# Keeping product 2's weights in dead activation tiles for product 3's sum, in the second projection of an FFN

## The chip, the cores and the metric

The kernel runs on one core of a Trainium2 chip. The metric is the device time of one execution in microseconds, as the median of several executions. Engines: PE (TensorE, with PEld for its weight loads), DVE (VectorE), ACT (ScalarE), POOL (GpSimd, used here to issue accumulating DMAs) and SP (SyncE, used here to issue DMAs).

## What is computed

A hybrid encoder trunk of two layers on 512 tokens of width 1024, all in float32. Each layer is a half-step FFN, a pair of gated mixers, and another half-step FFN; a final norm follows. Cut to what matters here:

```python
D_MODEL = 1024; SEQ = 512; DEPTH = 2; D_FF = 2816

def swiglu(x, w_in, w_out):
    gu = x @ w_in                      # 1024 -> 2 x 2816
    g, u = jnp.split(gu, 2, axis=-1)
    return (jax.nn.silu(g) * u) @ w_out  # 2816 -> 1024, "the second projection"

for l in range(DEPTH):
    x = x + 0.5 * swiglu(rms_norm(x, ffn1_norm[l]), ffn1_w_in[l], ffn1_w_out[l])
    x = x + mixer(rms_norm(x, mix_norm[l]), ...)
    x = x + 0.5 * swiglu(rms_norm(x, ffn2_norm[l]), ffn2_w_in[l], ffn2_w_out[l])
return rms_norm(x, final_norm)
```

There are four FFNs, called FFN 0 to FFN 3 here in the order in which they run.

## The kernel before

**Precision.** Every float32 operand is split into a high and a low part, and a product is three passes of matmuls: high by high, high by low, low by high (`mm3`, L509, L510 and L512). The split of a weight granule is `Item.prep`: ScalarE makes `whi` (L191, or L186 with a sign), VectorE makes `wlo` (L194, or L187). Both have three buffers. TensorE reads `whi` and `wlo` only.

**Strassen.** Each projection is a Strassen product of seven products, m = 1 to 7, out of weight quarters a, b, c, d. The weights lie in DRAM so that differences between quarters are formed on the way: product 1 reads a, 2 reads b, 4 reads d, and 5, 6, 7 and 3 read sums. `Raw.load` brings a granule of 128 x 1024 (512 KB; some are 256 KB) into a tile `raw` with a load on SyncE (L148). For the quarters c and d of products 5, 6, 7 and 3 a second, accumulating DMA on GpSimd adds another granule to the tile (L150): c += a, and d += c. `Item.summed` adds two tiles on VectorE (L164): a for product 6, b for product 3. The tiles `raw` come from a ring of nine.

**The stream of weights.** All granules of the kernel stand in one list in the order of use. `Stream.prep` splits a granule and, ahead of that, fetches up to `FETCH` = 8 granules further; TensorE's steps call `make(i)`, which prepares two granules ahead. So the place of a load in SyncE's queue follows from where the fetch stands when a step is issued, and a load for which no tile is free holds SyncE, and all that is queued behind it.

**The second projection.** It goes over the inner dimension in three chunks c = 0, 1, 2 of two granules each (chunk 0's second one is half as wide), in this order, where the last loop of `ffn()` lists the products:

```python
for order in ((1,), (2,), (5, 6, 7, 3), (4,)):
    for c in range(3):
        ...
        strassen(s, lambda q: "o" + q, c, out_sizes(c), order, summed)
```

That is product 1 of all chunks, product 2 of all chunks, then products 5, 6, 7, 3 of chunk 0, of chunk 1, of chunk 2, then product 4. In all 42 granules. The granule b of a chunk is read by product 2 and again, much later, by product 3, and is loaded for each of them. In FFN 3's chunk 2 (`summed`) the sum of product 3 is formed by an accumulating DMA into product 6's tile instead of by VectorE.

**Ahead of it.** The first projection runs in five blocks jb. Its last operand tiles are the normed activations, `xh` and `xl`, two tiles of each (`norm.h[0]`, `norm.h[1]`, `norm.l[0]`, `norm.l[1]`), each 128 x 4 x 512. The last block reads them for the last time in product 3 ("B" in the profile). The gated activations `z2`, and then `z1`, are turned so that they can be the second projection's operands. `halves` and `apart` do that: two copies on ScalarE into `zs` (L347), then a transposing DMA on SyncE into `zt` (L348). Later `joined` copies `zt` back into the words of `at` on ScalarE (L357), and the operands `c1h`, `c2h` and so on are split from `at` (L322 on ScalarE, L323 on VectorE). The step loop calls `joined` at step 3 and step 5: at step 3 for the second transposes (those of `z1`), at step 5 for the rest.

**After it.** The results update the residual x (L757). The next norm's tiles (`nxt`, again `xh` and `xl`) are begun at step 6 by `nxt.quad(0, 0)`, and filled further during product 4.

The set of engines' orders is written out by the program: an engine takes its instructions in the order of issue, except where the scheduler of the program framework moves them by priority.

Of the kernel before, what the change touches and what calls it, by code (L numbers as in the profile page):

```python
# [9 lines left out]
F32 = mybir.dt.float32  # L10
# [8 lines left out]
P = 128  # L19
D = 1024  # L20
T = 512
# [69 lines left out]
def encoder_kernel(  # L91
# [7 lines left out]
    np_ = ctx.enter_context(tc.tile_pool(name="np", bufs=1))  # L99
# [7 lines left out]
    def nm(s):  # L107
        uid[0] += 1
        return f"{s}_{uid[0]}"
# [27 lines left out]


    class Raw:
        def __init__(self, key, n=1024, plus=None):  # L140
            self.key, self.n, self.plus, self.t = key, n, plus, None

        def load(self, parts=1):
            if self.t is None:
                self.t = raw_pool[0](self.n)
                for c in range(0, self.n, self.n // parts):
                    cs = slice(c, c + self.n // parts)
                    nc.sync.dma_start(out=self.t[:, cs], in_=wst[GRAN_AT[self.key]][:, cs])  # L148
                if self.plus:
                    G.dma_start(out=self.t, in_=wst[GRAN_AT[self.plus]][:, 0 : self.n], accum_op=ALU.add)  # L150
# [48 lines left out]
    def stage_items():  # L199
        items, st = [], 0  # L200

        def add(*a, **k):
            items.append(Item(*a, stage=st, **k))

        def strassen(s, name, idx, sizes, order, dma=False, behind=None):
            def key(q, g):
                return (s, name(q), idx, g) if g < 2 else (s, "h" + q, idx, 0)

            r = {}
            for q, q2 in (("a", None), ("b", None), ("c", "a"), ("d", "c")):  # L210
                r[q] = [Raw(key(q, g), n, q2 and key(q2, g)) for g, n in enumerate(sizes)]
            d2 = [Raw(key("d", g), n) for g, n in enumerate(sizes)]
            at = [(m, g) for m in order for g in range(len(sizes))]
            if len(sizes) == 3:
                at.remove((2, 2))
                at.insert(at.index((7, 2)), (2, 2))
            for m, g in at:
                a, b, c, d = [r[q][g] for q in "abcd"]
                if m == 1:
                    add(a, neg=True)  # L220
                elif m == 2:
                    add(b)
                elif m == 3:
                    add(d, None if dma else b)
                elif m == 4:
                    add(d2[g])
                elif m == 5:
                    add(d)
                elif m == 6:
                    add(d, a, then=b.key if dma else None)  # L230
                else:
                    add(c)
                for key in (behind or {}).get(m, ()) if g == len(sizes) - 1 else ():
                    add(Raw(key))

        def out_sizes(c):
            return (1024, 512) if c == 0 else (1024, 1024)

        def ffn(s):
            first = not items  # L240
            if first:
                for g in range(4):
                    add(Raw((s, "cl", g)), parts=2 if g < 2 else 1, pieces=2 if g == 0 else 1)
            for j in range(NB):
                order = (1, 2, 5, 6, 7, 3, 4) if first and j == 0 else (1, 5, 6, 2, 7, 3, 4)
                strassen(s, lambda q: q, j, (1024,) * (2 if first or j else 3), order)
            for order in ((1,), (2,), (5, 6, 7, 3), (4,)):
                for c in range(3):
                    summed = s == (L - 1, 2) and c == 2
                    strassen(s, lambda q: "o" + q, c, out_sizes(c), order, summed)  # L250

        for l in range(L):
            ffn((l, 1))
            st += 1
            s = (l, 0)
            two = (1024, 1024)
            qk = [(s, "qk", g) for g in range(8)]
            strassen(s, lambda q: "u" + q, 0, two, (1, 5, 6, 2, 3, 7, 4), True, behind={5: qk[0:1], 6: qk[1:2], 2: qk[2:3], 3: qk[3:4], 7: qk[4:5]})
            for key in qk[5:] + [(s, "f", g) for g in range(4)]:
                add(Raw(key))  # L260
            st += 1
            for g in range(2):
                add(Raw((s, "n", 0, g)))
            st += 1
            for i in range(2):
                strassen(s, lambda q: "g" + q, i, two, ORDER, True)
            for g in range(2):
                add(Raw((s, "n", 1, g)))
            strassen(s, lambda q: "w" + q, 0, two, ORDER, True)
            ffn((l, 2))  # L270
        return items

    class Stream:
# [6 lines left out]
        def fetch(self, to):  # L280
            n = len(self.items)
            while self.loaded < min(to, n) and self.items[self.loaded].stage <= self.stage:
                self.items[self.loaded].load()
                self.loaded += 1

# [25 lines left out]

    ws = Stream()
    raw_pool = [None]

    def mm3(ps, lh, ll, rh, rl, start, stop, again=False):
        PE.matmul(ps, lh, rh, start=start, stop=False, skip_group_check=again)  # L316
        PE.matmul(ps, lh, rl, start=False, stop=False, skip_group_check=again)  # L317
        PE.matmul(ps, ll, rh, start=False, stop=stop, skip_group_check=again)  # L318
# [10 lines left out]
    def small(s, n=8):  # L329
        return sp.tile([P, 8], F32, tag=s, name=nm(s), bufs=2)[:, 0:n]  # L330
# [245 lines left out]
    def snap(ps):  # L576
        t = slot(F32, "sn", (2, T))
        for b in range(2):
            S.activation(t[:, b, :], ps[b], AF.Copy)  # L579
        return t  # L580
# [35 lines left out]
    def stage_ffn(norm, nxt, late):  # L616
# [127 lines left out]
        def hl(src, c, s):  # L744
            n = len(CHUNK[0][c])
            h, l = slot(F32R, s + "h"), slot(F32R, s + "l")
            split(h[:, 0:n, :], l[:, 0:n, :], src)
            return h, l, 0
# [24 lines left out]
        def make(i):  # L773
            if i < len(steps) and i not in made:
                m, c, f = steps[i]
                made[i] = hl(f(), c, f"c{m}")
# [95 lines left out]
        for jb in range(0 if first else 1, NB):  # L872
            f0 = 2 + 4 * jb
            if first and jb == 0:
                with tc.manual_schedule(engines={mybir.EngineType.DVE, mybir.EngineType.Activation}):
                    pa = pair("A")
                    product(pa, acts[1], K4, True)
                    for j in range(2):
                        t = snap(pcl[j])
# [37 lines left out]

        if late or nxt.mix:
            tc.keep_in_program_order(S.activation(small("sq", 1), ones, AF.Sqrt))
        ps = {}  # L920
        for i, (m, c, _) in enumerate(steps):
            make(i)
# [2 lines left out]
            key = {6: 1, 4: 7}.get(m, m)  # L925
# [17 lines left out]
            if m == 4 and c == 0 and not late:  # L943
                with tc.manual_schedule(engines={mybir.EngineType.DVE, mybir.EngineType.Activation}):
# [4 lines left out]
                    else:  # L949
                        nxt.quad(0, 1)  # L950
            make(i + 2)
            if i == 6 and not late:
                nxt.quad(0, 0)
            if m == 4 and c == (0 if late else 1):
# [67 lines left out]
    ob = {}  # L1022
# [830 lines left out]
    for l in range(L):  # L1853
        nxt = Norm(3 * l + 1)
        stage_ffn(norm, nxt, False)
        norm, nxt = nxt, Norm(3 * l + 2)
        stage_mixer(l, norm, nxt)
        norm, nxt = nxt, Norm(3 * l + 3)
        stage_ffn(norm, nxt, l == L - 1)
        norm = nxt  # L1860
# [139 lines left out]
```

## Time and profile before

| | |
|---|---|
| Time, three runs | 1854.66, 1856.72, 1858.52 us; median 1856.72 |
| The profiled execution | 1854.76 us; span from the first to the last instruction 1853.0 us |
| Granted TensorE clock | 0.999 |
| DMA | 394.21 MB, mean 213 GB/s |
| Loads of weights on SyncE | 468 of 512 KB, 30 of 256 KB |
| Accumulating DMAs on GpSimd | 176 of 512 KB, 8 of 256 KB |

A row of a timeline has the start in us from the beginning of the span, the duration, the engine, the line, the operation, output and inputs, the count where alike instructions follow each other, and in brackets the engine's idle time just before and what ended it. A row on a line or tile gives the count, the shortest, median and longest duration in ns, and the first and the last start. "DMA to landing" is the time from a DMA's issue until its data have arrived. A DMA instruction on SyncE (SPq) takes the engine's time until it has been handed on, which for a transposing DMA can be long.

### The profile page before, as it was taken

The numbers are of one execution on the slowest core, as the hardware profiler recorded it, in microseconds if no ns is written. First come the engines' busy times: TensorE is split into PE (matmuls) and PEld (weight loads), VectorE is DVE, ScalarE is ACT, GpSimd is POOL, SyncE is SP. The second block draws the span as 40 slices with busy tenths as digits, with TensorE's granted clock in tenths as the row PEclk, the third lists the DMA queues.
The fourth block names the chain that finished last, engine by engine and source line by source line (L and its number), as shares of the span: only waits on it lengthen the run. The fifth ranks groups of instructions, "written<-read, shape, count | busy, mean of one in ns | idle before, by whom it ended". The sixth has DMA issues, their size and how long they took to land.

```text
span 1853.0 us, 24606 instructions
## 1 busy us (share of the span) xinstructions
PE 1840.1 (99%) x8862; PEld 1530.2 (83%) x8862; DVE 1602.5 (86%) x1946; ACT 1311.3 (71%) x1781; POOL 173.1 (9%) x212
## 2 busy tenths in 40 slices
PE   9999999999999999999999999999999999999998
PEld 7888888888888888887888888888888888888886
DVE  7878899886989987889998878998869899888898
ACT  6777876668576777777667777766675776777865
POOL 0001010100101001001010000101001101010010
PEclk9999999999999999999999999999999999999999
DMA  9898799933886788979888887988249867888795
GB/s 308 220 249 206 193 272 273 226 96 109 242 235 175 183 219 229 207 200 264 247 197 222 213 216 204 280 273 212 71 145 238 226 181 173 230 221 208 216 284 146
DMA packets 198602, 394.21 MB, mean 213 GB/s; under 512 B 103824, under 2 KB 103952, under 8 KB 198480
## 3 DMA queue, kind: packets, MB, share of 16 engines
q1 hardware_dynamic: 169232, 292.72, 49.3%
q0 software_dynamic: 28816, 99.38, 29.9%
q8 instruction: 69, 1.13, 0.3%
q10 hardware_dynamic: 432, 0.55, 0.1%
q14 instruction: 53, 0.43, 0.1%
HBM read 365.85 MB, written 2.11 MB: 199 GB/s over the span
## 4 chain that ended last, share of the span: by engine, by line
PE 93%; DVE 3%; DMA 2%; issue 2%; ACT 1%; POOL 0%; SPq 0%; DVEq 0%; ACTq 0%; POOLq 0%
PE A L509 10%; PE A L512 10%; PE A L510 10%; PE o L509 7%; PE o L512 7%; PE o L510 7%; PE B L510 5%; PE B L509 5%; PE B L512 5%; PE ps L316 4%; PE ps L317 3%; PE ps L318 3%; PE C L509 2%; PE C L510 2%; PE C L512 2%
## 5 line engine op out<-in xcount | busy, mean ns | idle before, releaser
L194 DVE TENSOR_TENSOR wlo<-raw,whi 128x1024 fp32r<-128x1024 f32 (+1 forms) x534 | 630.6, 1191 | 174.2 <-ACT whi L191 173.0
L191 ACT ACTIVATE whi<-raw 128x1024 fp32r<-128x1024 f32 (+1 forms) x534 | 545.7, 1033 | 254.3 <-DVE raw L164 56.8
L150 POOL DMA_DIRECT2D raw<-in_wst_dram x166 | 144.3, 889 | 1336.8 <-DMA raw<-in_wst_dram 850.1
L164 DVE TENSOR_TENSOR raw<-raw,raw 128x1024 f32<-128x1024 f32 (+1 forms) x148 | 176.1, 1191 | 2.0
L510 PE MATMUL A<-whi,xl 128*128 128x512 f32 x400 | 155.7, 389 | 0.0
L509 PE MATMUL A<-whi,xh 128*128 128x512 f32 x400 | 155.7, 389 | 0.0
L357 ACT ACTIVATE at<-zt 128x1024 uint16<-128x1024 uint16 (+2 forms) x96 | 110.2, 1166 | 20.4 <-DMA zt<-zs 20.4
L186 ACT ACTIVATE whi<-raw 128x1024 fp32r<-128x1024 f32 (+1 forms) x83 | 86.0, 1036 | 46.6 <-issue 12.5
L512 PE MATMUL A<-wlo,xh 128*128 128x512 f32 x400 | 115.0, 389 | 0.0
L187 DVE SCALAR_TENSOR_TENSOR wlo<-raw,whi 128x1024 fp32r<-128x1024 f32 (+1 forms) x83 | 98.2, 1191 | 11.3 <-ACT whi L186 11.3
L512 PEld LDWEIGHTS A<-wlo,xh 128*128 128x128 f32 x400 | 75.1, 188 | 15.6
L510 PEld LDWEIGHTS A<-whi,xl 128*128 128x128 f32 x400 | 75.1, 188 | 15.4
L509 PEld LDWEIGHTS A<-whi,xh 128*128 128x128 f32 x400 | 75.1, 188 | 15.4
L509 PE MATMUL C<-whi,xh 128*128 128x512 f32 x208 | 81.1, 390 | 0.9 <-ACT whi L191 0.9
L510 PE MATMUL C<-whi,xl 128*128 128x512 f32 x208 | 81.0, 389 | 0.0
L510 PE MATMUL B<-whi,xl 128*128 128x512 f32 x208 | 81.0, 389 | 0.0
L509 PE MATMUL B<-whi,xh 128*128 128x512 f32 x208 | 80.9, 389 | 0.0
L347 ACT ACTIVATE zs<-th 128x1024 uint16<-128x1024 uint16 x80 | 79.4, 1041 | 0.9 <-DVE th L738 0.9
L731 ACT ACTIVATE th<-sn,rh 128x512 f32<-128x512 f32 x80 | 55.1, 715 | 34.6 <-DVE sn L584 33.8
L579 ACT ACTIVATE sn<-A 128x512 f32<-128x512 f32 x104 | 59.1, 585 | 24.8 <-PE A L512 24.8
L512 PE MATMUL B<-wlo,xh 128*128 128x512 f32 x208 | 59.8, 389 | 0.0
L512 PE MATMUL C<-wlo,xh 128*128 128x512 f32 x208 | 59.8, 389 | 0.0
(438 smaller groups left out, 4679.5 us busy)
## 6 DMA issues: line engine op xcount, KB each, us to landing
raw<-in_wst_dram SPq DMA_DIRECT2D x468, 512.0 KB, 5.6
raw<-in_wst_dram POOLq DMA_DIRECT2D x176, 512.0 KB, 7.8
raw<-in_wst_dram SPq DMA_DIRECT2D x30, 256.0 KB, 4.1
bm<-in_bias_dram SPq DMA_DIRECT2D x16, 384.0 KB, 3.7
x<-in_xin_dram SPq DMA_DIRECT2D x4, 512.0 KB, 10.2
raw<-in_wst_dram POOLq DMA_DIRECT2D x8, 256.0 KB, 9.1
dft<-in_dft_dram POOLq DMA_DIRECT2D x8, 256.0 KB, 4.4
gb<-in_gbias_dram SPq DMA_DIRECT2D x4, 512.0 KB, 15.5
```

The costliest lines, as they stand in the source:

```text
L150: G.dma_start(out=self.t, in_=wst[GRAN_AT[self.plus]][:, 0 : self.n], accum_op=ALU.add)
L164: V.tensor_tensor(self.raw.t, self.raw.t, self.add.t, ALU.add)
L186: S.activation(hi, t, AF.Copy, scale=-1.0)
L187: self.last = V.scalar_tensor_tensor(lo, t, -1.0, hi.bitcast(F32), ALU.mult, ALU.subtract)
L191: S.activation(hi[:, cs], t[:, cs], AF.Copy)
L194: self.last = V.tensor_tensor(lo[:, cs], t[:, cs], hi[:, cs].bitcast(F32), ALU.subtract)
L316: PE.matmul(ps, lh, rh, start=start, stop=False, skip_group_check=again)
L347: S.activation(s[:, h], words[:, h], AF.Copy)
L357: S.activation(to[:, w], t[:, w], AF.Copy)
L509: PE.matmul(ps, lh, rh, start=start, stop=False, skip_group_check=again)
L510: PE.matmul(ps, ll, rh, start=False, stop=False, skip_group_check=again)
L512: PE.matmul(ps, lh, rl, start=False, stop=stop, skip_group_check=again)
```

## The change

Product 2's granules of chunks 1 and 2, four of 512 KB, are no longer loaded into the ring of `raw` tiles. They go into two tiles that take the places of `xh[1]` and `xl[1]`, two granules in each. Product 3's sums of these chunks read them there, so the second load of b for product 3 falls away. That is four loads less in each of FFN 0, 1 and 2, and two less in FFN 3, where chunk 2's sum is formed by DMA. The tiles are made just ahead of the step loop (`homes[0]`); until then the fetch stops at the first such granule, and from step 6 on no more can be placed.

Two orders follow from it. The kept granules use no tile of the ring, so loads behind them in the list are issued sooner. On SyncE the order around the second transposes becomes: four kept loads, the two d of chunk 0, the first transposes, the two a, the first c, the second transposes, the second c. Before it was: the four loads of product 2, the first transposes, the two d, the second transposes, the two a, the two c. GpSimd's order is the same as before, but its accumulating DMAs of chunk 0's d wait for loads that now stand ahead of the first transposes. On ScalarE and VectorE the sixth split of product 1 moves behind the second copies `zs`, and in FFN 1 one split of product 2 moves behind the copies `at`. TensorE's instructions and their order are unchanged.

The granules are those that product 2 read before (keys "ob"), and the data in DRAM are unchanged.

```diff
     class Raw:
-        def __init__(self, key, n=1024, plus=None):
-            self.key, self.n, self.plus, self.t = key, n, plus, None
+        def __init__(self, key, n=1024, plus=None, home=None):
+            self.key, self.n, self.plus, self.home, self.t = key, n, plus, home, None
 
         def load(self, parts=1):
             if self.t is None:
-                self.t = raw_pool[0](self.n)
+                self.t = homes[0](*self.home) if self.home else raw_pool[0](self.n)
...
-        def strassen(s, name, idx, sizes, order, dma=False, behind=None):
+        def strassen(s, name, idx, sizes, order, dma=False, behind=None, kept=None):
...
+            if kept:
+                r["b"] = kept
...
+            kept = [c and [Raw((s, "ob", c, g), home=(c, g)) for g in range(2)] for c in range(3)]
             for order in ((1,), (2,), (5, 6, 7, 3), (4,)):
                 for c in range(3):
                     summed = s == (L - 1, 2) and c == 2
-                    strassen(s, lambda q: "o" + q, c, out_sizes(c), order, summed)
+                    strassen(s, lambda q: "o" + q, c, out_sizes(c), order, summed, kept=kept[c])
...
             while self.loaded < min(to, n) and self.items[self.loaded].stage <= self.stage:
+                if self.items[self.loaded].raw.home and not homes[0]:
+                    break
                 self.items[self.loaded].load()
...
     raw_pool = [None]
+    homes = [None]
...
+        kept = [np_.tile([P, 4, T], F32, tag=t, name=nm("ob"), bufs=2) for t in ("xh", "xl")]
+        homes[0] = lambda c, g: kept[c - 1][:, 2 * g : 2 * g + 2, :].rearrange("p k t -> p (k t)")
         ps = {}
         for i, (m, c, _) in enumerate(steps):
...
             make(i + 2)
+            if i == 6:
+                homes[0] = None
```

## The prediction

> **What bounds the kernel now.** I read the page's busy shares and chain first, then the waits of TensorE, then the stage of the change alone: the timelines of SyncE, ScalarE and VectorE there, and the windows of the same stretch in each of the four FFNs.
>
> ```profile
> PE 1840.1 (99%) x8862; PEld 1530.2 (83%) x8862; DVE 1602.5 (86%) x1946; ACT 1311.3 (71%) x1781; POOL 173.1 (9%) x212
> PE 93%; DVE 3%; DMA 2%; issue 2%; ACT 1%; POOL 0%; SPq 0%; DVEq 0%; ACTq 0%; POOLq 0%
> L164 DVE TENSOR_TENSOR raw<-raw,raw 128x1024 f32<-128x1024 f32 (+1 forms) x148 | 176.1, 1191 | 2.0
> raw<-in_wst_dram SPq DMA_DIRECT2D x468, 512.0 KB, 5.6
> ```
>
> TensorE is busy 99% of the span, and the change touches none of its instructions. So whatever happens is small, and comes from TensorE being made to wait more or less. The waits of TensorE (total, times, longest) say where it waits now:
>
> ```profile
> PE o L509 <- ACT whi L191: 1.0, 1, 1.0
> PE C L509 <- ACT whi L191: 0.9, 1, 0.9
> PE o L512 <- DVE wlo L194: 0.8, 2, 0.6
> ```
>
> None of these is a wait for a weight's transfer: the weights are there, and what is sometimes late is their split into a high and a low part by ScalarE and VectorE. Two of the three lines are in the second projection ("o"). VectorE is the engine with no room there. The windows show it (columns: stretch, its length, then busy us of PE, PEld, DVE, ACT, POOL, the granted clock, the DMA share, GB/s). They are the first 15 or 16 us after the second transposes, in FFN 0, 1, 2 and 3 in that order, and then the rest of FFN 0's projection:
>
> ```profile
> 235.00:250.00 15.00, 15.00 (x68) 12.40 (x67) 14.21 (x15) 13.16 (x15) 2.17 (x3) 1.00 0.99 261
> 833.00:849.00 16.00, 14.99 (x66) 12.07 (x65) 12.97 (x14) 13.35 (x14) 1.72 (x2) 1.00 0.84 224
> 1156.00:1171.00 15.00, 15.00 (x68) 12.43 (x67) 14.21 (x15) 13.15 (x15) 1.73 (x2) 1.00 0.95 253
> 1754.00:1769.00 15.00, 15.00 (x68) 12.43 (x67) 14.20 (x16) 13.20 (x14) 1.75 (x2) 1.00 0.93 245
> 250.00:283.00 33.00, 33.00 (x151) 27.43 (x150) 32.69 (x34) 22.17 (x29) 4.74 (x6) 1.00 1.00 282
> 283.00:311.00 28.00, 28.00 (x125) 23.02 (x124) 27.94 (x30) 16.30 (x20) 2.27 (x3) 1.00 0.90 285
> ```
>
> VectorE is idle for 0.8 us in three of the FFNs at that place and for 3.0 us in FFN 1 (16.00 less 12.97), and there TensorE loses 1.0 us in the window. After it VectorE works without a gap: 32.69 of 33 us and 27.94 of 28. What it loses near 239 it can hardly make up before the projection ends.
>
> What the idle time waits for is the second transposes (`zt`), through ScalarE's copies `at<-zt`:
>
> ```profile
> L348 SPq DMA_TRANSPOSE zt<-zs x1: 3751/3751/3751, 229.0 to 229.0; - x1
> DMA to landing us min/median/max: 5.7/5.7/5.7
> 235.51 2.57 ACT L357 ACTIVATE at<-zt 128x1024 uint16<-128x1024 uint16 x2
> 239.01 1.23 DVE L194 TENSOR_TENSOR wlo<-raw,whi 128x1024 fp32r<-128x1024 f32 x1 [0.79 <-ACT whi L191]
> L348 SPq DMA_TRANSPOSE zt<-zs x1: 3026/3026/3026, 826.9 to 826.9; - x1
> DMA to landing us min/median/max: 7.5/7.5/7.5
> 834.53 2.57 ACT L357 ACTIVATE at<-zt 128x1024 uint16<-128x1024 uint16 x2 [4.49 <-DMA zt<-zs]
> 838.03 1.23 DVE L194 TENSOR_TENSOR wlo<-raw,whi 128x1024 fp32r<-128x1024 f32 x1 [2.95 <-ACT whi L191]
> 214.14 1.06 ACT L186 ACTIVATE whi<-raw 128x1024 fp32r<-128x1024 f32 x1 [1.47 <-PE B L510]
> 812.14 1.06 ACT L186 ACTIVATE whi<-raw 128x1024 fp32r<-128x1024 f32 x1 [1.47 <-PE B L510]
> ```
>
> In FFN 0 the transposes land at 229.0+5.7 = 234.7, and the copies start at 235.51 with no idle time before them: 0.8 us to spare. In FFN 1 they land at 834.4, ScalarE has stood 4.49 us, and VectorE then stands 2.95. The last two rows are the projection's first split in both, 598.0 us apart, so FFN 1's landing is 236.4 on FFN 0's clock. The rule I take from the pair, on FFN 0's clock: a landing up to 235.5 costs nothing, and each us beyond it delays VectorE by a us.
>
> **The change part by part.**
>
> *Loads removed.* Product 2's weights of chunks 1 and 2 are four granules of 512 KB, loaded a second time for product 3's sum. The second load goes: 4 in each of FFN 0 to 2, and 2 in FFN 3, whose chunk 2 sums by DMA. 14 loads, 7.3 of 394 MB. SyncE and the transfers are not what ends last (chain: SPq 0%), so this removes nothing from the path directly. The DMA share is 0.90 to 1.00 in FFN 0's windows, so fewer transfers may bring others in sooner, but TensorE has no wait for one. Bounds: 0, and the 2.95 us that FFN 1 loses to a late transfer. I take 0.5 us, near zero, because the four removed loads of an FFN belong to product 3, far behind the one transfer that is late.
>
> *Sums.* Fourteen of the 148 sums of L164 read their second operand from another tile, same shape: 1191 ns before and after. Nothing.
>
> *The kept tiles wait for TensorE.* They take the place of `xh[1]` and `xl[1]`, read last by the last "B" product:
>
> ```profile
> 237.94 1.03 ACT L191 ACTIVATE whi<-raw 128x1024 fp32r<-128x1024 f32 x1
> ```
>
> The split at 214.14, which waited for that product's matmuls ("PE B" in its bracket), marks about when the tiles are free; the row above is the split of the first kept granule, the projection's ninth. Between them lie 24 us for a transfer of 5.6 us. Nothing on this path. The next norm's tiles take the kept tiles' places only after product 3's sums, which lie ahead of it anyway: nothing.
>
> *SyncE's order.* This is the step that counts. Kept granules take no place in the ring of nine, so the fetch runs four granules further at the same moment, and the loads for products 5 and 6 come forward past the transposes. SyncE before:
>
> ```profile
> 212.37 10.44 SPq L148 DMA_DIRECT2D raw<-in_wst_dram  x5
> 222.90 4.94 SPq L348 DMA_TRANSPOSE zt<-zs  x1
> 227.94 1.01 SPq L148 DMA_DIRECT2D raw<-in_wst_dram  x2
> 229.03 3.75 SPq L348 DMA_TRANSPOSE zt<-zs  x1
> 232.88 28.48 SPq L148 DMA_DIRECT2D raw<-in_wst_dram  x13
> ```
>
> After, by the order of instructions: four kept loads, `d` and `d'` of chunk 0, first transposes, `a`, `a'`, `c`, second transposes, `c'`. So the second transposes are moved behind three loads (1.25 MB) instead of two, and, what weighs more, GpSimd's accumulating DMAs `d += c` and `d' += c'` are moved too. They run at 232.8 now, behind both transposes; with `d` and `d'` ahead of the first transposes they run at about 223, beside them. What a transpose costs behind two accumulates is to be seen in the fourth FFN's main loop:
>
> ```profile
> L150 POOL DMA_DIRECT2D raw<-in_wst_dram x2: 860/902/945, 232.8 to 233.6; - x2
> DMA to landing us min/median/max: 8.0/8.7/9.4
> L150 POOL DMA_DIRECT2D raw<-in_wst_dram x2: 851/854/856, 1583.9 to 1585.0; - x2
> L348 SPq DMA_TRANSPOSE zt<-zs x1: 6637/6637/6637, 1586.7 to 1586.7; - x1
> DMA to landing us min/median/max: 8.7/8.7/8.7
> ```
>
> With accumulates issued 1.7 to 2.8 us ahead the transposes held SyncE for 6.6 us, not the 4.9 of 222.90 or the 3.8 of 229.03. So: first transposes at 222.9 (ScalarE's copies set that, unchanged), SyncE free at 222.9+6.6 = 229.5; three loads at 0.5 each (two took 1.01), 231.0; second transposes then land 5.7 later, at **236.7**. The nearest ends: 222.9+4.9+1.5+5.7 = 235.0 if accumulates do not hold the first transposes, and 231.0+7.5 = 238.5 if the second take what FFN 1's do. I take the middle, as 5.7 was measured with two loads just ahead and the accumulates will be through by then.
>
> The Trainium skill, page "DMA: Bandwidth & Descriptors", section "Queues, rings and completion order", says that an engine goes round robin between the rings it has work for, a packet at a time. By it the transposes would share with the accumulates and not stand behind them. The row of 6.6 us speaks against full independence; the rival it gives is below.
>
> *ScalarE's order.* The sixth of product 1's splits moves behind the copies `zs` and the table load; TensorE needs it long after. The `zs` come 1 us sooner, hidden as SyncE is busy until 231. Nothing.
>
> *The sum*, with the landing at 236.7: the copies start 1.2 to 1.3 us late in FFN 0. What can absorb it on the way to the end of the projection:
>
> ```profile
> 268.72 1.23 DVE L194 TENSOR_TENSOR wlo<-raw,whi 128x1024 fp32r<-128x1024 f32 x1 [0.31 <-ACT whi L191]
> 307.39 1.22 DVE L194 TENSOR_TENSOR wlo<-raw,whi 128x1024 fp32r<-128x1024 f32 x1
> 308.69 0.70 PE L512 MATMUL o<-wlo,c3h 128*128 128x512 f32 x2
> ```
>
> 0.3 us of idle time, and 0.1 us between the end of a low part (308.61) and the matmuls that read it (308.69). So 1.3-0.4 = 0.9 us in FFN 0. FFN 2 has the same window, 0.9. FFN 3 has the same first gap, but an estimate of 0.2, since its last chunk has no sums on VectorE and so more room. FFN 1 lands at 236.4 already, its 7.5 falls to 5.7 when the accumulates go first and its issue comes as much later: +0.2. Together 0.9+0.9+0.2+0.2-0.5 = **+1.7 us**. The profiled execution took 1854.76 us (span 1853.0); it becomes 1856.5. The median of the three runs is 1.96 above it, so 1858.4 as a median.
>
> **The rivals.** Measurements of this kernel can tell about 0.2% from no change, 3.7 us: below 1853.0 is faster, above 1860.4 slower.
>
> *Slower: the second transposes land past 237.2.* Both transposes and three more loads stand behind two accumulates, and each of the four FFNs pays. At 237.7: FFN 0 and 2 lose 2.2-0.4 = 1.8 each, FFN 3 some 1.4 (0.8 absorbed), FFN 1 1.3 (237.7 less 236.4), together 6.3-0.5 = +5.8, 1862.5. At 238.5 it is 2.6+2.6+2.2+2.1-0.5 = +9.0, 1865.7. It decides from 237.2 on. For it speaks FFN 1's 7.5 us at the same place; against, that the accumulates have a start of 8 us. Chance 0.27.
>
> *Shared service.* The accumulates take nothing from the first transposes' time, the landing is 235.0, three FFNs lose nothing, and FFN 1 gains 236.4-235.0 = 1.4, with 0.5: -1.9, 1854.8. For it: 4.9 us at 222.90. Against: 6.6 at 1586.7. This is the page's rule as a mechanism here. Chance 0.13.
>
> *Faster: the late transposes cease to be late.* With the accumulates through, and 2 MB of product 3's loads gone, they land by 233.5 on FFN 0's clock, all of FFN 1's 2.95 us go: -3.0-0.5 = -3.5, 1853.2. Against it stands that they are issued later, not sooner. Chance 0.07.
>
> *It has no effect at all*, as the three loads pass ahead in SyncE's idle time and the accumulates wait for something else: 1856.7, 0.05. That the loads would not really go is out: the order of instructions shows 14 fewer.
>
> **How the numbers follow.** The forecast, a landing between 235.5 and 237.2 and a time from 1855.5 to 1860.6, has the remaining 0.48. Faster by over 0.2%: 0.06 of shared service, 0.05 of the fast rival, 0.01 of no effect, 0.12. Slower: 0.23 of the slow rival and 0.10 of the forecast's upper edge, 0.33. Same: 0.55. The range runs from the fast rival's 1853.2 to 1863.5, between the slow rival's two prices, which leaves about 1 in 10 at each end.
>
> **What the profile after would show.** Right: 454 loads of 512 KB on SyncE, accumulates of chunk 0 at about 223, the first transposes holding SyncE for over 6 us, second transposes landing near 236.7 in FFN 0, and VectorE's idle time before L194 at 239 near 2.1 us instead of 0.79. Wrong: a landing of FFN 0's second transposes before 235.5 or past 237.2, TensorE waiting for a transfer or for a sum of L164 in product 3, or first transposes still at 4.9 us with accumulates beside them.

## The result, and the profile after

The changed kernel took 1863.55 us (median of 6 runs, 1862.99 to 1864.21), the kernel before 1857.58 us (6 runs, 1852.67 to 1859.28). The ratio is 1.0046, 95% interval 1.0033 to 1.0058: slower by 0.46%, which is 8.5 us; the two medians differ by 6.0 us. The profiled execution went from 1854.76 to 1863.31 us, its span from 1853.0 to 1861.5.

The page after, its busy line and its chain, and the waits of TensorE (lines lie 6 further down in this file, so L515, L518 and L354 are the old L509, L512 and L348; in the experiments' files they lie a few further again):

```profile
PE 1843.7 (99%) x8862; PEld 1531.7 (82%) x8862; DVE 1602.6 (86%) x1946; ACT 1311.6 (70%) x1781; POOL 173.1 (9%) x212
PE 94%; DVE 3%; DMA 2%; issue 1%; ACT 1%; SPq 0%; DVEq 0%; ACTq 0%
PE o L515 <- ACT whi L191: 4.6, 2, 4.0
PE o L518 <- DVE wlo L194: 2.5, 3, 1.0
```

No engine has more work than before. TensorE waits 7.1 us in the second projection ("o") where it waited 1.8 us, and for the same two things as before, the split of a weight granule on ScalarE and on VectorE. SyncE's timeline of FFN 0 and the second transposes with GpSimd's two accumulates, to be held against 229.03, 3.75 and 5.7 before:

```profile
214.22 1.75 SPq L148 DMA_DIRECT2D ob<-in_wst_dram  x4
216.07 1.31 SPq L148 DMA_DIRECT2D raw<-in_wst_dram  x2
222.69 2.87 SPq L354 DMA_TRANSPOSE zt<-zs  x1
225.66 1.81 SPq L148 DMA_DIRECT2D raw<-in_wst_dram  x3
227.57 8.48 SPq L354 DMA_TRANSPOSE zt<-zs  x1
...
L354 SPq DMA_TRANSPOSE zt<-zs x1: 8478/8478/8478, 227.6 to 227.6; - x1
DMA to landing us min/median/max: 10.6/10.6/10.6
...
L150 POOL DMA_DIRECT2D raw<-in_wst_dram x2: 860/860/860, 224.4 to 226.6; - x2
DMA to landing us min/median/max: 8.0/8.9/9.7
```

The order is the predicted one. The second transposes are issued 1.5 us sooner than before and land 3.4 us later, at 238.1 instead of 234.8. They held SyncE until 236.1, and about then the transfers that were issued ahead of them are in: the last of the three loads at 236.3, the later accumulate at 236.4. In the other three FFNs the last load lands 0.2 to 0.3 us after SyncE is free, and the later accumulate 1.1 to 1.7 us before that load.

What follows on ScalarE and VectorE, and the windows of the same stretch of FFN 0 to 3:

```profile
238.20 2.58 ACT L363 ACTIVATE at<-zt 128x1024 uint16<-128x1024 uint16 x2 [2.52 <-DMA zt<-zs]
241.71 1.22 DVE L194 TENSOR_TENSOR wlo<-ob,whi 128x1024 fp32r<-128x1024 f32 x1 [3.41 <-ACT whi L191]
...
235.00:250.00 15.00, 14.94 (x66) 11.79 (x65) 11.59 (x12) 12.48 (x14) 2.58 (x3) 1.00 0.89 202
834.00:850.00 16.00, 12.03 (x42) 9.41 (x41) 9.64 (x11) 11.25 (x11) 2.58 (x3) 0.79 0.89 212
1160.00:1176.00 16.00, 16.00 (x71) 13.01 (x70) 12.91 (x15) 13.41 (x14) 2.56 (x3) 1.00 0.90 214
1760.00:1776.00 16.00, 15.26 (x66) 11.97 (x65) 11.81 (x13) 12.48 (x13) 2.58 (x3) 1.00 0.92 201
```

VectorE's idle time is 3.4 us in FFN 0 (0.8 before), 6.4 in FFN 1 (3.0), 3.1 in FFN 2 (0.8) and 4.2 in FFN 3 (0.8).

The stage of a second projection is measured here, from the timelines, from the start of the first matmul that reads `c1h` to the start of the first that reads `c4h`. All runs are in one table, in us, with the times:

| kernel | FFN 0 | FFN 1 | FFN 2 | FFN 3 | median | ratio to before (95%) |
|---|---|---|---|---|---|---|
| before | 90.8 | 93.7 | 90.7 | 89.8 | | |
| after | 92.9 | 97.5 | 92.6 | 92.3 | 1863.55 | 1.0046 (1.0033 to 1.0058) |
| all behind | 90.9 | 90.7 | 90.7 | 89.8 | 1850.45 | 0.9982 (0.9973 to 0.9991) |
| before, turned | 92.0 | 92.3 | 91.2 | 91.0 | 1852.79 | 0.9996 (0.9986 to 1.0006) |
| transposes last | 94.5 | 100.5 | 93.5 | 91.9 | 1867.35 | 1.0075 (1.0063 to 1.0088) |
| loads behind | 90.7 | 92.7 | 90.7 | 89.8 | 1851.90 | 0.9988 (0.9979 to 0.9996) |
| sums behind | 90.7 | 92.3 | 90.7 | 89.8 | 1850.89 | 0.9987 (0.9978 to 0.9995) |
| loaded twice | 92.9 | 96.7 | 92.3 | 90.9 | 1873.81 | 1.0111 (1.0097 to 1.0124) |
| all behind, loaded twice | 90.7 | 90.7 | 90.7 | 89.8 | 1859.98 | 1.0037 (1.0024 to 1.0051) |
| all behind, same place | 92.2 | 92.0 | 92.1 | 90.3 | 1854.57 | 1.0010 (1.0001 to 1.0019) |
| FFN 1's order | 93.0 | 93.3 | 93.2 | 91.2 | 1859.54 | 1.0034 (1.0021 to 1.0047) |

Where TensorE waits for nothing in it, the stage takes 90.7 to 90.9 us, and 89.8 in FFN 3. Where the transposes are late it varies between executions: FFN 3 took 92.3, 90.9 and 91.2 us in the changed kernel, in "loaded twice" and in "FFN 1's order", whose order around the transposes is the same there. A difference of 1 us between two such stages tells little.

The medians were taken beside runs of the kernel before at 1857.58, 1854.32 (four kernels), 1853.30 (four) and 1853.33 us, so kernels of different groups are compared by their ratios. Against the kernel before, the four stages of the changed kernel lose 2.1+3.8+1.9+2.6 = 10.4 us. The rest of the kernel gains 1.9, of which 0.9 is a wait of TensorE before FFN 2's projection that this execution does not have, and the span is 8.5 us longer.

### The profile page after: what moved, and what is told of

It is laid out like the page before. It is cut to its first block, busy times and chain, and to the rows that moved or that the text cites. A ratio compares the mean times of both kernels' runs of the same rounds, so it can differ in the third digit from the quotient of the medians.

```text
span 1861.5 us, 24565 instructions
## 1 busy us (share of the span) xinstructions
PE 1843.7 (99%) x8862; PEld 1531.7 (82%) x8862; DVE 1602.6 (86%) x1946; ACT 1311.6 (70%) x1781; POOL 173.1 (9%) x212
## 4 chain that ended last, share of the span: by engine, by line
PE 94%; DVE 3%; DMA 2%; issue 1%; ACT 1%; SPq 0%; DVEq 0%; ACTq 0%
PE A L515 10%; PE A L518 10%; PE A L516 10%; PE o L518 6%; PE o L515 6%; PE o L516 6%; PE B L515 5%; PE B L516 5%; PE B L518 5%; PE ps L322 4%; PE ps L323 3%; PE ps L324 3%; PE C L515 3%; PE C L516 3%; PE C L518 3%; DMA zt<-zs 2%
## 5 line engine op out<-in xcount | busy, mean ns | idle before, releaser
L194 DVE TENSOR_TENSOR wlo<-raw,whi 128x1024 fp32r<-128x1024 f32 (+1 forms) x518 | 611.1, 1189 | 164.3 <-ACT whi L191 163.5
L191 ACT ACTIVATE whi<-raw 128x1024 fp32r<-128x1024 f32 (+1 forms) x518 | 529.2, 1033 | 252.8 <-PE A L516 54.3
L164 DVE TENSOR_TENSOR raw<-raw,raw 128x1024 f32<-128x1024 f32 (+1 forms) x134 | 159.0, 1187 | 2.0
L515 PE MATMUL A<-whi,xh 128*128 128x512 f32 x400 | 155.7, 389 | 0.0
L186 ACT ACTIVATE whi<-raw 128x1024 fp32r<-128x1024 f32 (+1 forms) x83 | 85.7, 1034 | 45.6 <-issue 12.5
L518 PE MATMUL A<-wlo,xh 128*128 128x512 f32 x400 | 115.0, 389 | 0.0
L187 DVE SCALAR_TENSOR_TENSOR wlo<-raw,whi 128x1024 fp32r<-128x1024 f32 (+1 forms) x83 | 98.5, 1192 | 11.4 <-ACT whi L186 10.3
L518 PEld LDWEIGHTS A<-wlo,xh 128*128 128x128 f32 x400 | 75.1, 188 | 15.6
L515 PEld LDWEIGHTS A<-whi,xh 128*128 128x128 f32 x400 | 75.1, 188 | 15.4
L515 PE MATMUL C<-whi,xh 128*128 128x512 f32 x208 | 81.1, 390 | 0.0
L515 PE MATMUL B<-whi,xh 128*128 128x512 f32 x208 | 80.9, 389 | 0.0
L518 PE MATMUL B<-wlo,xh 128*128 128x512 f32 x208 | 59.8, 389 | 0.0
L518 PE MATMUL C<-wlo,xh 128*128 128x512 f32 x208 | 59.8, 389 | 0.0
```

What stands on the lines that cost most here:

```text
L164: V.tensor_tensor(self.raw.t, self.raw.t, self.add.t, ALU.add)
L186: S.activation(hi, t, AF.Copy, scale=-1.0)
L187: self.last = V.scalar_tensor_tensor(lo, t, -1.0, hi.bitcast(F32), ALU.mult, ALU.subtract)
L191: S.activation(hi[:, cs], t[:, cs], AF.Copy)
L194: self.last = V.tensor_tensor(lo[:, cs], t[:, cs], hi[:, cs].bitcast(F32), ALU.subtract)
L518: PE.matmul(ps, lh, rl, start=False, stop=stop, skip_group_check=again)
```

## The experiments

The theory T after the prediction: the accumulates, now beside the transposes, hold them. R1: the three loads ahead of the second transposes do. R2: the kept tiles themselves cost the time.

**All behind.** Only SyncE's order is changed: every load behind the four kept ones is queued after both transposes (`turn[0]` holds the second ones when the step loop begins).

```diff
-        nc.sync.dma_start_transpose(
+        turn[0] = nc.sync.dma_start_transpose(
...
+        hold[:] = turn[0].ins, ws.pos + 12
         ps = {}
...
-                self.items[self.loaded].load()
+                behind = hold[0] is not None and self.loaded >= hold[1]
+                with tc.issue_after(hold[0]) if behind else nullcontext():
+                    self.items[self.loaded].load()
```

> The changed kernel, but in each FFN every load after the four kept ones (the d, a and c of products 5 to 7) is queued on SyncE behind both transposes; nothing else moves on any engine. Theory T (GpSimd's accumulates of d hold the second transposes) and rival R1 (the three loads ahead of them do) both expect the second transposes of FFN 0 to be issued near 227.5 and to land at 231 to 234, VectorE's idle time at 239 to be 0.8 us, and FFN 1 to lose its 3 us less: 1853.5 to 1855.5 us, 2 to 4 us below the kernel before. Rival R2 (the kept tiles themselves, their loads in one burst after the last B product or their place) expects the loss to stay: 1861 to 1864 us.

Measured: 0.9982 of before, 3.3 us faster than it and, by the two ratios (1.0046 over 0.9982), 0.64% or 12 us faster than the changed kernel (by the medians, each against the runs of the kernel before beside it, 10 us). The 3.3 us lie within the 2 to 4 us that T and R1 expected, and the stages put them in one place, FFN 1, which goes from 93.7 to 90.7. Nothing else than SyncE's order separates the two. Its second transposes, its TensorE waits (the whole list) and the window of FFN 1:

```profile
L357 SPq DMA_TRANSPOSE zt<-zs x1: 2155/2155/2155, 227.6 to 227.6; - x1
DMA to landing us min/median/max: 4.6/4.6/4.6
...
PE ps L136 <- DVE ones L132: 1.2, 1, 1.2
PE wC L519 <- DVE m2l L332: 0.2, 1, 0.2
...
833.00:849.00 16.00, 16.00 (x72) 13.28 (x71) 15.97 (x18) 12.27 (x14) 3.93 (x5) 1.00 1.04 265
```

With nothing ahead they land 4.6 us after their issue, at 232.2. TensorE waits for nothing in any second projection. R2 is out: the kept tiles cost no time here.

**Before, turned.** The same edit to the kernel before: the two d behind both transposes.

> The kernel before, with the two loads of d queued on SyncE behind both transposes instead of between them. All theories: the second transposes are issued some 1 to 1.5 us sooner and land by 233.5 on FFN 0's clock in all four FFNs, FFN 1's idle time of 2.95 us shrinks to about 0.8: 1854 to 1856 us. The difference to the run with the kept tiles and the same order is what the 14 loads are worth; I expect 0 to 1 us.

Measured: 0.9996, no change that can be told. FFN 1 gains 1.4 us (93.7 to 92.3), but the other three stages lose 1.2, 0.5 and 1.2. The stages are those of the longest of its eleven runs (1857.89 us, 5 us above the median), so they may overstate the loss. Some waits come later in the stage: in FFN 0 VectorE stands at 279.66, in FFN 1 ScalarE at 878.19. That the cause is transfers that come later now is shown by the second row alone; ahead of the first, ScalarE waited for TensorE:

```profile
279.66 1.23 DVE L194 TENSOR_TENSOR wlo<-raw,whi 128x1024 fp32r<-128x1024 f32 x1 [1.50 <-ACT whi L191]
878.19 1.06 ACT L191 ACTIVATE whi<-raw 128x1024 fp32r<-128x1024 f32 x1 [2.71 <-DMA raw<-in_wst_dram]
```

So turning the order alone brings nothing, and keeping the tiles with the order turned brings 3.3 us. The two medians, run side by side, differ by 2.3 us, where 0 to 1 us was expected; the intervals of their ratios overlap slightly.

**Loads behind.** Only a, a' and c go behind the second transposes; the accumulates of d run beside them. Against the edit of "all behind":

```diff
-        hold[:] = turn[0].ins, ws.pos + 12
+        hold[:] = turn[0].ins, ws.pos + 14
```

> The changed kernel with only a, a' and c queued behind the second transposes; d, d' stay ahead of the first, so GpSimd's accumulates run beside the transposes. T: the second transposes still hold SyncE for 6 us or more and land past 236 in FFN 0: 1860 to 1863.5 us. R1: they land at 232 to 234 and the time is 1854 to 1856 us. R2: 1861 to 1864 us.

**Sums behind.** SyncE's order is that of the changed kernel; GpSimd's accumulates of chunk 0 wait for the second transposes' data.

```diff
-                    G.dma_start(out=self.t, in_=wst[GRAN_AT[self.plus]][:, 0 : self.n], accum_op=ALU.add)
+                    g = G.dma_start(out=self.t, in_=wst[GRAN_AT[self.plus]][:, 0 : self.n], accum_op=ALU.add)
...
+                        tc.add_manual_dep(
+                            g.ins, hold[0].name,
...
+        hold[:] = turn[0].ins, 4
```

> The changed kernel with SyncE's order as changed (d, d', first transposes, a, a', c, second transposes), and GpSimd's accumulates of chunk 0's d and c waiting until the second transposes have landed. So only the three loads are ahead of them, no accumulate. If the transposes wait for every transfer that is already under way (what the three runs so far suggest: held until the last earlier one lands, then about 2 us), FFN 0's land at 232.5 to 235 and the time is 1850.5 to 1854 us: neither the accumulates alone (234.7, no loss) nor the loads alone cost anything, only both. Rival: the loads are the whole cost, they land past 236, 1858 to 1864 us.

The second transposes of the two kernels, and the accumulates of the first:

```profile
L357 SPq DMA_TRANSPOSE zt<-zs x1: 5332/5332/5332, 227.4 to 227.4; - x1
DMA to landing us min/median/max: 7.3/7.3/7.3
...
L150 POOL DMA_DIRECT2D raw<-in_wst_dram x2: 860/860/860, 224.1 to 226.3; - x2
DMA to landing us min/median/max: 6.7/6.9/7.2
...
L362 SPq DMA_TRANSPOSE zt<-zs x1: 5077/5077/5077, 228.8 to 228.8; - x1
DMA to landing us min/median/max: 7.3/7.3/7.3
```

Accumulates alone ahead: landing at 234.7. Loads alone ahead: at 236.1, in an execution whose projection starts 1.4 us later (221.3 against 219.9), so 234.7 as well. Both ahead: 238.1; neither: 232.2. Each costs 2.5 us, both together 5.9, and ScalarE wants the data at 235.5. So each alone is free in FFN 0, 2 and 3 (90.7, 90.7, 89.8 in both kernels), and only together they are late. T's expectation of the first of these runs fell. R1's came nearer, but the landing, 234.7, is past its 232 to 234; R1 falls with the second run, where the three loads are ahead and nothing is lost in these stages. The second run came out as its first reading expected: it takes both. FFN 1 keeps 92.7 and 92.3 in the two, against 90.7 with nothing ahead; there ScalarE wants the data earlier (it stands 2.2 and 1.7 us for them).

**Transposes last.** This kernel was meant as the run above, but the edge ran the other way: the second transposes are issued only after both accumulates have landed (the later one at 235.2 in FFN 0). Its expectation speaks of the order that was meant:

> The changed kernel with SyncE's order unchanged (d, d', first transposes, a, a', c, second transposes), but GpSimd's two accumulates of chunk 0's d wait until the second transposes have landed. T: the second transposes land at 233 to 234.5 in FFN 0, as without accumulates beside them, and the time is 1854 to 1856.5 us. R1: three loads of 1.25 MB ahead of them are what counts, they still land past 236.5, and the time stays at 1861 to 1864 us. R2: 1861 to 1864 us too.

```profile
L362 SPq DMA_TRANSPOSE zt<-zs x1: 1839/1839/1839, 235.3 to 235.3; - x1
DMA to landing us min/median/max: 4.3/4.3/4.3
```

It tells no theory apart, but it prices the transposes by themselves: 1.8 us on SyncE and 4.3 to the landing, as in the kernel with nothing ahead. And it shows how near the changed kernel is to a full wait: 239.6 here, 238.1 there.

**FFN 1's order.** ScalarE's copies `at<-zt` behind the split of the first kept granule, in FFN 1 alone, as the other FFNs have it. In FFN 1 that split stands behind the copies in the kernel before, too; what the change moves there is that the operand `c2h` is made ahead of the split. The rows: FFN 0 of the changed kernel, whose copies start at 238.20; FFN 1 of the kernel before, with its copies at 834.53; FFN 1 of the changed kernel, with its copies at 838.39.

```profile
234.62 1.06 ACT L191 ACTIVATE whi<-ob 128x1024 fp32r<-128x1024 f32 x1 [1.59 <-PE o L516]
...
836.97 1.03 ACT L191 ACTIVATE whi<-raw 128x1024 fp32r<-128x1024 f32 x1
837.90 1.04 ACT L322 ACTIVATE c2h<-at 128x1024 fp32r<-128x1024 f32 x1
...
840.96 1.06 ACT L328 ACTIVATE c2h<-at 128x1024 fp32r<-128x1024 f32 x1
841.92 1.04 ACT L191 ACTIVATE whi<-ob 128x1024 fp32r<-128x1024 f32 x1
```

```diff
-                    S.activation(hi[:, cs], t[:, cs], AF.Copy)
+                    self.high = S.activation(hi[:, cs], t[:, cs], AF.Copy)
...
-                joined()
+                with tc.issue_after(ws.items[ws.pos].high.ins) if norm.idx == 2 else nullcontext():
+                    joined()
```

> The changed kernel with one order changed in FFN 1 alone: ScalarE's copies at<-zt come behind the split of the first kept granule, as in the other three FFNs. The second transposes land late as before (838.3). If FFN 1's stall of 4 us and the clock of 0.60 after it come from that order, the stall falls to about 1 us, the clock stays at 1.00, and FFN 1's stage takes 92.5 to 93 us as in FFN 0 and 2 instead of 97.5: 1858 to 1860.5 us. Rival: the landing alone sets FFN 1's loss, then the time stays at 1862 to 1864 us.

Measured: 1.0034 against the changed kernel's 1.0046, 2 us by the ratios, whose intervals overlap, and 4 us by the medians, as expected. The stage is clearer than the total: FFN 1's goes from 97.5 to 93.3 though its transposes still are late, and the other three stay late too. Some later splits and sums of FFN 1 change places as well, far behind the stall. TensorE's wait for `whi` in the projections falls from 4.6 us to 0.5. Changed kernel first, its clock and its matmuls after the stall, then this kernel:

```profile
838.65 0.39 PE L518 MATMUL o<-wlo,c2h 128*128 128x512 f32 x1
843.02 0.80 PE L515 MATMUL o<-whi,c2h 128*128 128x512 f32 x1 [3.97 <-ACT whi L191]
843.61 0.63 PE L516 MATMUL o<-whi,c2l 128*128 128x512 f32 x1
843.00:850.00 7.00, 6.98 (x19) 5.57 (x20) 6.73 (x8) 6.68 (x7) 0.86 (x1) 0.60 0.58 146
...
PE o L515 <- ACT whi L191: 0.5, 2, 0.3
842.00:849.00 7.00, 6.65 (x29) 4.85 (x28) 6.23 (x6) 7.00 (x8) 0.86 (x1) 1.00 0.73 190
```

**Loaded twice, three ways.** The 14 loads come back, the kept tiles stay. First in the changed kernel, then in the kernel with all loads behind, each time into the ring; last into the kept tiles themselves. The edit of the first two:

```diff
+            b3 = [Raw(key("b", g), n) for g, n in enumerate(sizes)] if kept else r["b"]
...
-                    add(d, None if dma else b)
+                    add(d, None if dma else b3[g])
```

> The changed kernel, but product 3's b of chunks 1 and 2 is loaded a second time into the ring, so the kept tiles serve product 2 alone and all 14 loads are back; orders around the transposes as changed. If the loss is all in the order at the transposes and the loads that fall away are worth what the pair with good order says (2.3 us), 1864.5 to 1867 us; if the loads are worth nothing behind late transposes, 1863 to 1864.5.

> The kernel with all loads of products 5 to 7 behind both transposes, but product 3's b of chunks 1 and 2 loaded a second time: what the 14 loads are worth when the transposes are in time. If the 2.3 us between that kernel and the kernel before with turned order are the loads' (transfers that come marginally late to product 3 and 4), 1852.5 to 1854 us, and VectorE's idle times of 0.8 to 1.5 us some 60 and 90 us into the stage come back; if they are the ring's (four tiles more at the start of the stage), 1850 to 1851.5 us.

> The kernel with all loads of products 5 to 7 behind both transposes, with the 14 loads of product 3's b back, but into the kept tiles themselves (the same data again, into the same place, before the sums). No place of the ring is used, and no order changes on any engine but SyncE. So it adds only 7.3 MB of transfers. If the loads themselves are worth something in this stage, the stages grow beyond 90.9 us and the time is 1852 to 1854 us; if only the four places of the ring are, the stages stay at 90.7 (89.8 in FFN 3) and the time at 1850 to 1851.5 us.

The totals of the first two, 1.0111 and 1.0037, lie above both readings of their expectations, and they do not price the loads: the stages are no longer than without them (92.9, 96.7, 92.3, 90.9 beside 92.9, 97.5, 92.6, 92.3; and 90.7, 90.7, 90.7, 89.8 beside 90.9, 90.7, 90.7, 89.8). The time is lost at the start of the mixers, after FFN 0 and after FFN 2. In the second kernel, and, for comparison, in the one with all loads behind:

```profile
PE B L519 <- ACT t5h L619: 3.6, 2, 1.8
L1083 POOL DMA_DIRECT2D ch<-in_chan_dram x1: 555/555/555, 321.5 to 321.5; - x1
  DMA bm<-in_bias_dram: 32.7, 1
...
L1082 POOL DMA_DIRECT2D ch<-in_chan_dram x1: 555/555/555, 311.6 to 311.6; - x1
```

GpSimd's load of `ch` is issued 10 us later, when a bias transfer is in, and the mixers' first accumulates stand behind it. TensorE then stands 1.8 us in each mixer, and the clock is 0.50 for some 3 us after it (from 337.3 in the first). Why that load waits so with four more tiles taken from the ring was not tried. The third kernel takes none, and there the loads cost 5 us by the ratios and 4 by the medians, 1.2 to 1.4 us in each of three stages and 0.6 in FFN 3, as the first reading of its expectation has it. They come in one burst, from 238.8 to 245.4 in FFN 0, and the loads behind them are issued from 250.2 on; later ScalarE stands for a transfer and VectorE behind it (1.8 us at 270.75). So what the loads are worth depends on where they stand: nothing in the stage where they come late, 4 to 5 us where they come in a burst. The 2.3 us against the turned kernel before lie between; they hold the loads and the four free places of the ring together, and these two were not separated.

## Why the prediction was wrong, and where it was right

**Right.** The bound and the place: TensorE's instructions are untouched, and all that counts is when the second transposes land, ScalarE's copies behind them, and VectorE with no room after. The order on SyncE came out as read, and the loads needed on the way to product 2 wait for nothing. The rule from landing to loss held too: with 238.1 it gives 238.2-235.5-0.4 = 2.3 us for FFN 0, and the stage lost 2.1; FFN 2 lost 1.9, FFN 3 2.6. What happened is the slow rival, a landing past 237.2. That its price, +9.0 at a landing of 238.5, is so near the measured +8.5 is in part luck: FFN 1 lost 3.8 where it has 2.1, and outside the stages 1.9 were gained where it has 0.5.

One reading does not hold, and nothing hangs on it: the split at 237.94 is that of the second kept granule. The first one's is at 234.54, which leaves 20 us, not 24, for its transfer.

**Wrong: the landing, 236.7 predicted, 238.1 measured.** The step that failed is which transposes the accumulates hold. They were put ahead of the first, and the second were given 5.7 us because the accumulates "will be through by then". The prediction's own rows speak against that: issued at about 223 with 8.0 to 9.4 us to their landing, they land at 231.0 to 232.4, and the second transposes were to be issued at 231.0. In the changed kernel the accumulates are issued at 224.4 and 226.6, when the first transposes are under way (222.69, 2.87 us on SyncE, not 6.6). So SyncE was free earlier than predicted, the second transposes were issued at 227.6 and not at 231.0, and right into both accumulates and three loads: 10.6 us to the landing. The two errors have opposite signs, 3.4 us sooner and 4.9 us longer, and what is left is 1.4 us in FFN 0. FFN 0, 2 and 3 lost 2.1, 1.9 and 2.6 us against +0.9, +0.9 and +0.2 in the sum. The end of 238.5 was in the working, and by those rows it was the one to take.

**Wrong: FFN 1, +0.2 predicted, +3.8 measured.** The step that failed is "its 7.5 falls to 5.7": it rose to 11.0. The landing, 838.3, is 238.4 on FFN 0's clock, as FFN 1's stage starts 599.9 us after FFN 0's, and that is 2.0 us past the 236.4 of before. The rest is ScalarE's order. The next weight split stands behind the late copies there, as it did before, but `c2h` now comes ahead of it too, and the splits after it follow one place later. (The move that the section on the change names is the last of these: product 2's last split at 847.90, behind the second copies at 845.50.) None of this was priced. So TensorE stood 4.0 us, until 843.02, where it had stood 1.0, and the clock fell. With the split ahead of the copies the stage is 4.3 us shorter (97.5 to 93.3).

**Mis-sized: the loads removed, 0.5 us taken.** With the transposes in time the kept tiles are worth about 2.3 us, loads and free places of the ring together, and the argument for "near zero", that no wait of TensorE names a transfer, looked one step too short: the transfers show up as ScalarE's wait, then as VectorE's, and only then as TensorE's. The fast rival's -3.5 is close to what the kernel with all loads behind gained (-3.3), and by its mechanism, FFN 1's transposes in time; but the order had to be made by hand. The sum, +1.7, stands against a measured +8.5: 2.1+3.8+1.9+2.6 in the stages, -1.9 outside of them.

**The shared-service rival** fell in its form here: the transposes did not pass the accumulates. In the kernel with only accumulates ahead they hold SyncE until 227.4+5.3 = 232.7, and the accumulates land at 231.3 and 233.0. The transposes move their data in packets of under 512 B, the loads and accumulates nearly all of theirs in larger ones. Of these small packets 53 start from 227.4 to 231 us and 2083 from 231 to 234.7 us:

```profile
DMA packets 214, 0.57 MB, mean 157 GB/s; under 512 B 53, under 2 KB 53, under 8 KB 213
DMA packets 2178, 0.75 MB, mean 202 GB/s; under 512 B 2083, under 2 KB 2083, under 8 KB 2178
```

By the Trainium skill, page "DMA: Bandwidth & Descriptors", section "Queues, rings and completion order", an engine takes turns between its rings a packet at a time; these rows, in which the transposes land 1.7 us after the last earlier transfer, do not show such sharing between a transpose and what was issued ahead of it.

## What to carry to other kernels

A transfer that takes no place in a ring any more lets everything behind it in its queue start sooner, and that includes transfers that then stand in front of something urgent. It is the place that does it, not the load that falls away: with the 14 loads back ("loaded twice") FFN 0's second transposes still took 10.3 us to land. So read where a freed place in a ring sends the queue, and fix the order of the urgent transfer by hand before judging the change. Here the same edit is 0.46% slower with the order that came by itself and 0.18% faster with the transposes first. Two transfers that each fit into the slack can be late together: add up everything under way at the moment of issue, not the one that looks most likely.

## What the runs showed of the hardware

A transposing DMA on SyncE holds that engine until about the time when the transfers issued ahead of it are in, on whichever queue they were, and lands behind them: 1.7 to 2.7 us after the last of them for the second transposes of the changed kernel. That makes 4.6 and 4.3 us to the landing with nothing ahead, 7.3 with two accumulates, 7.3 with three loads, 10.6 with both. Accumulates issued behind it, while it still holds SyncE, seem to delay its landing too. In FFN 1 of the kernel before they were issued 2.2 and 3.0 us behind the second transposes, whose last earlier transfer was in at 829.3; they landed at 834.4, 5.1 us later. With those loads and accumulates moved away ("before, turned") the 7.5 us became 4.5. No run moved the accumulates alone.

A stall of TensorE can cost more than its length. After the stall of 4.0 us in FFN 1 the granted clock was 0.60 over the next 7 us and matmuls came every 0.43 us instead of 0.23. That is 2.8 us of the full clock lost besides the 4.0, and the stage is 6.9 us longer than in the kernel with all loads behind. In the kernel with transposes last, after a stall of 6.3 us, the clock was 0.60 again (first row). In its FFN 0 a stall of 1.6 us was enough: the matmuls ran on, and from 245.0 to 248.4 the clock was 0.50 (second and third row). A stall of 1.1 us, elsewhere in the kernel with loads behind, left it at 1.00 (last two rows):

```profile
847.00:854.00 7.00, 7.00 (x19) 5.53 (x20) 6.73 (x8) 6.61 (x7) 0.86 (x1) 0.60 0.77 142
243.20 0.50 PE L523 MATMUL o<-whi,c2h 128*128 128x512 f32 x1 [1.59 <-ACT whi L198]
245.00:248.40 3.40, 3.40 (x9) 2.67 (x8) 3.40 (x4) 3.40 (x5) 0.86 (x1) 0.50 0.96 264
1678.09 0.50 PE L518 MATMUL C<-whi,xh 128*128 128x512 f32 x1 [1.14 <-ACT whi L191]
1678.00:1685.00 7.00, 6.91 (x30) 5.74 (x31) 4.19 (x4) 7.00 (x10) 0.00 (x0) 1.00 0.48 150
```

So did 0.3 us in FFN 1 of the kernel with FFN 1's order (842.00:849.00 above), and 1.0 us in FFN 1 of the kernel before (its window 833.00:849.00). The Trainium skill, page "TensorE: Matmul & The Clock Gate", section "Part 1: The HAM clock gate (the "warmup" mystery)", puts the limit at about one idle window of 3.4 us, after which the clock is halved until some 3.4 us of work have passed. The halving agrees with the 0.50 here. The limit does not: a stall of 1.6 us, less than half that figure, was followed by the slow clock. In these runs, once the kernel is under way, the longest single stall that left the clock alone took 1.1 us; whether the limit depends on when a stall falls, no run here shows.
